# Join of first stage, attention and output projection: conditioning rows, casts and multiplications moved between engines in a two-layer hybrid backbone

## The chip, the core and the metric

The kernel runs on one core of one Trainium2 chip. The core has five engines, each with its own instruction stream: TensorE (PE) multiplies matrices and loads their stationary operands (PEld), VectorE (DVE) does element-wise work and reductions, ScalarE (ACT) does copies, casts and activation functions, GpSimd (POOL) does element-wise work too, and SyncE (SP) mostly starts transfers (DMA). The engines wait for each other through semaphores. The metric is the device time of one execution in microseconds (us), as the median over runs.

## The reference

The function is a two-layer backbone over 2048 latent tokens (a grid of 32 x 64) and 256 context tokens, 1024 channels wide. Cut to what matters here, one layer is:

```python
shift, scale, gate = jnp.split(silu(c) @ w_ada[l] + b_ada[l], 3, axis=-1)   # conditioning, latent and context
hx = rmsnorm(x, norm_w[l]) * (1.0 + scale) + shift
(fx, fgx, nq, nk, nv, ng, gq, gk, gv, gg, zf, zb) = jnp.split(hx @ w_in[l], IN_SPLITS, axis=-1)
four_x = fourier_mix(fx, w_four[l])                       # 4 groups, real part of a 2-D DFT, a linear map
na_x = neighbourhood_attention(nq, nk, nv, nkc, nvc, rpb) # 6 heads, window 8 x 16, and all context keys
gla_x = ...                                               # 4 heads of gated linear attention, both directions
mix_x = concatenate([four_x * silu(fgx), na_x * silu(ng), gla_x * silu(gg)])
x = x + gate * (mix_x @ w_out[l])
```

Context tokens go through the same weights with their own conditioning in the first layer. A last RMSNorm follows the second layer. All inputs are float32. The kernel works in pairs of float16 numbers instead: a value is split into its rounded half (high) and the rest (low), and a product is the sum of the multiplications of the halves.

## The kernel before, in words

**Stages.** A layer has a Fourier stage, an attention stage (`na`), a stage of gated linear attention and an output projection. Weights and conditioning of later stages are prepared in small steps in between. In the first layer a start-up comes ahead of them (from L1660 on): it computes the conditioning, normalises the tokens, two tiles of 128 tokens (a *pair*) at a time, and multiplies each pair by the first two groups of the input weights, `fx` (values of the Fourier group) and `fg` (their gate).

**Order.** Nearly all instructions are issued through `Pin` (L64), which keeps an engine's instructions in the order in which the program issues them; L72 is its line, so nearly every row of a profile bears L72, and instructions are told apart by the names of their tiles. The order of the code is thus the order on each engine, and an engine waits at the instruction whose operand is late, with all later ones behind it.

**Banks.** PE writes into banks of 128 x 512 numbers, of four kinds with two buffers each, named `b_a`, `b_b`, `b_c` and `b_pj`.

**Conditioning (`ada`, L131).** The product `silu(c) @ w_ada` is done in chunks of 256 columns, each with its own weight block of 1 MB. For a chunk PE does eight multiplications, one for each 128 input channels, with a stationary operand of two columns (latent and context), `sil`. They lie in four groups of rows of one bank, 0, 32, 64 and 96, two rows each, so the result is the sum over four groups of rows. In the start-up `mm_r` does the multiplications and `fin_r` the rest: ACT copies the first two rows to `ada_row`, DVE adds the other three groups, PE transposes the row into columns by two small multiplications with `ident`, and DVE adds the bias columns `bc`. In the first layer's attention stage the same is done for the second layer by `chunk`: there the steps are `s0` (loads of weights and of the bias row), `s1` (multiplications), `s1b` (four DVE additions) and `s2` (transposes and a copy). Chunks 0 to 7 give shift and scale; chunks 8 to 11 give the gate and are stored as rows.

**Weights (`w_steps`, L468).** A group of input weights is prepared in steps: a load, four reductions to the largest magnitude (`red`), a multiplication by `dg` that spreads this maximum over all rows (`mm`, `top_b`), its reciprocal (`inv`), and then four slices each of the high and the low halves (`hi` on ACT, `lo` on DVE). `sc` says whether the factors that depend on the conditioning are computed at the end as well.

**A pair in the start-up.** `norm_a` squares and sums on ACT, `norm_b` scales the tokens, `put_t` turns them with 16 small multiplications by `ident` into the banks b and c, and `put_e` evacuates these with the conditioning into `hu`, on ACT and at two of eight places on DVE, then splits `hu` into the high (DVE) and low (POOL or DVE) halves of `hx`. `four_x` and `four_g` multiply `hx` by a group of weights, 48 multiplications a pair of the first size.

**Attention.** A *unit* is a pair of heads and a block of 512 latent queries (or the 256 context queries): three head pairs, with five blocks in the first layer and four in the second, 27 units in all. A unit is a list of steps that `fill` (L889) puts in order: each step gets a due time between 0 and 1 and the list is sorted by it. In a unit stand, among others:

- the scores of each piece, `score`: multiplications `b_a<-q,k` and `b_a<-Q,K`, a DVE step that adds the position bias (`pt`), and behind it, as `flush` in the list, the exponential on ACT (`pt<-pt,psh`), its cast to the high half `ph` on ACT and the low half `pl` on POOL; then `value`, the multiplications `b_c<-ph,vt` and `b_c<-pl,vt`;
- for the next unit the projection of the queries and `st_q`, whose `cast` makes the high halves on DVE and the low halves `q` on POOL;
- for the next unit the row maxima `st_m`: multiplications `k,q` in the banks a and b, a DVE maximum `MX` each, then the maxima's halves `mh`, and in `fin` (L729) 16 small multiplications with `mh` into a bank b, which are cast into two query operands `Q`, 64 x 512 each: the first (h = 0) on ACT, the second (h = 1) on DVE;
- for the unit before its `tail` (L757): the reciprocals of the row sums with three transfers (`rc<-rs`, `rrd<-rc`, `rs<-rrd`), and as its last step two POOL multiplications, `gt<-gt,rs` and `ob<-ob,gt`, and a store;
- side jobs (`side`): weights of later groups, the second layer's conditioning in the first layer, and `wo_scale`, the maximum of the output weights.

## Time and profile before

| what | value |
|---|---|
| median of 3 runs | 2481.02 us (2479.67 to 2491.21) |
| the profiled execution's own time | 2481.09 us |
| its span in the trace | 2479.3 us |
| mean granted clock of PE | 0.979 of full speed |
| instructions of PE, DVE, ACT, POOL | 16878, 3625, 2049, 1285 |

The durations in the rows further down come from one profiled execution, whose time lies 0.07 us from the median. Busy time is the time in which an engine works on an instruction; PE's loads of stationary operands run beside its multiplications and are counted apart. A multiplication's end is modelled, so rows of PE can overlap by fractions of a microsecond. The granted clock says at which share of full speed PE ran in a stretch: 1.0 is 2.4 GHz, 0.5 is 1.2 GHz.

### The profile page before, as it was taken

To read this page: it belongs to the slowest core of one execution; us is meant where nothing else is said; L and a number is where in the kernel's file an instruction comes from. 1 tells how busy PE (TensorE), PEld (TensorE's weight loads), DVE (VectorE), ACT (ScalarE), POOL (GpSimd) and SP (SyncE) were. 2 spreads that over 40 slices of the span, in tenths; PEclk is the share of its full clock that TensorE was granted. 3 is DMA by queue.
4 is the path that set the end of the run, shared out by engine and by line. 5 is a ranking of instruction groups with operands and counts; after the bars stand their busy time and mean duration, and the time that the engine had idled before them with its cause. 6 is when DMAs were issued, how large, how long until landed. Compare 5 with 4: busy or idle time off the path is not lost.

```text
span 2479.3 us, 44404 instructions
## 1 busy us (share of the span) xinstructions
PE 2308.9 (93%) x16878; PEld 1540.2 (62%) x16878; DVE 1623.3 (65%) x3625; ACT 1121.3 (45%) x2049; POOL 1123.5 (45%) x1285
## 2 busy tenths in 40 slices
PE   5999998999978999999999999999999799999998
PEld 3555454454546999895444644555555599989443
DVE  5765766676766666696774627667666666679554
ACT  3623554555555444342332225566666534434222
POOL 1524444455544444454553143655555444445343
PEclk7999999999999999999999999999999999999999
DMA  6304124124221110264443021131320211036442
GB/s 256 119 1 137 64 82 114 62 86 125 75 88 59 44 39 31 99 197 160 145 145 119 19 89 32 46 100 52 83 56 24 73 41 38 31 98 208 147 149 98
DMA packets 128622, 225.05 MB, mean 91 GB/s; under 512 B 18724, under 2 KB 81816, under 8 KB 122776
## 3 DMA queue, kind: packets, MB, share of 16 engines
q1 hardware_dynamic: 123224, 212.58, 25.1%
q0 software_dynamic: 5184, 9.64, 2.6%
q8 instruction: 133, 2.18, 0.4%
q14 instruction: 81, 0.66, 0.1%
HBM read 176.79 MB, written 51.37 MB: 92 GB/s over the span
## 4 chain that ended last, share of the span: by engine, by line
PE 36%; DVE 7%; ACT 3%; issue 2%; POOL 1%; DMA 1%; POOLq 0%; SPq 0%; ACTq 0%; DVEq 0%
PE b_pj L72 18%; PE b_a L72 8%; PE b_c L72 4%; PE b_pj L313 3%; PE b_b L72 2%; DVE ot L72 1%; DVE pt L72 1%; ACT pt L72 1%; DVE SU L72 0%; PE b_a L374 0%; DMA rc<-rs 0%; DVE wo L72 0%; DVE w L72 0%; ACT ph L72 0%; DVE gt L72 0%
## 5 line engine op out<-in xcount | busy, mean ns | idle before, releaser
L72 PE MATMUL b_pj<-hx,w 128*128 128x512 f16 (+1 forms) x3168 | 690.0, 364 | 1.8 <-DVE w L72 0.9
L72 POOL TENSOR_TENSOR pl<-pt,ph 128x512 f16<-128x512 f32 (+6 forms) x300 | 306.6, 1024 | 444.2 <-ACT ph L72 368.7
L72 PEld LDWEIGHTS <-w 128*128 128x128 f16 x3168 | 305.6, 99 | 277.1 <-issue 15.8
L72 PEld LDWEIGHTS <-hx 128*128 128x128 f16 x5088 | 435.6, 99 | 5.5
L72 PE MATMUL b_pj<-w,hx 128*128 128x192 f16 (+2 forms) x4272 | 391.4, 250 | 0.0
L72 PE MATMUL b_pj<-wo,m 128*128 128x512 f16 x816 | 302.7, 380 | 0.0
L72 PE MATMUL b_a<-wo,m 128*128 128x512 f16 x816 | 302.4, 380 | 0.0
L72 PEld LDWEIGHTS <-m 128*128 128x128 f16 x1632 | 160.1, 98 | 184.5 <-issue 1.6
L72 DVE SCALAR_TENSOR_TENSOR pt<-b_a,sc,TS 128x160 f32<-128x160 f32 (+4 forms) x432 | 153.0, 400 | 136.9 <-PE b_a L72 99.9
L72 ACT ACTIVATE pt<-pt,psh 128x480 f32<-128x480 f32 (+1 forms) x192 | 121.6, 633 | 169.1 <-DVE pt L72 156.7
L72 PE MATMUL b_c<-ph,vt 128*128 128x320 f16 (+5 forms) x888 | 179.4, 294 | 3.2 <-ACT ph L72 3.2
L72 PEld LDWEIGHTS <-vt 128*128 128x128 f16 x1332 | 120.7, 100 | 94.6 <-issue 31.7
L72 POOL TENSOR_TENSOR xn<-xn,xt 128x512 f32<-128x512 f32 x66 | 110.3, 1692 | 149.0 <-DVE xn L72 117.6
L72 ACT CAST ph<-pt 128x512 f16<-128x512 f32 (+6 forms) x300 | 166.5, 555 | 9.5
L72 PE MATMUL b_c<-pl,vt 128*128 128x320 f16 (+5 forms) x444 | 126.4, 294 | 9.7 <-POOL pl L72 9.6
L72 PE MATMUL b_a<-Q,K 128*128 128x320 f16 (+5 forms) x444 | 120.7, 294 | 13.1 <-ACT Q L72 13.1
L72 DVE CUSTOM_DVE_ANT_0 b_b<-b_b,tmi 128x512 f32<-128x512 f32 (+3 forms) x144 | 86.4, 600 | 69.5 <-PE b_b L72 68.9
L72 PE MATMUL b_a<-q,k 128*128 128x320 f16 (+5 forms) x444 | 121.2, 295 | 4.7 <-DVE MX L72 2.3
L72 ACT ACTIVATE pt<-b_a,psh,sc 128x512 f32<-128x512 f32 (+1 forms) x108 | 81.1, 750 | 78.7 <-PE b_a L72 67.9
L72 PEld LDWEIGHTS <-q 128*128 128x128 f16 x540 | 51.0, 98 | 81.9 <-issue 21.1
L72 POOL TENSOR_TENSOR ats<-ATm 128x512 f32<-128x512 f32 x34 | 43.3, 1272 | 126.9 <-DVE ATm L72 126.9
L313 PE MATMUL b_pj<-hx,w 128*128 128x512 f16 x432 | 96.8, 379 | 0.0
(272 smaller groups left out, 4212.1 us busy)
## 6 DMA issues: line engine op xcount, KB each, us to landing
mx<-mixd SPq DMA_DIRECT2D x34, 512.0 KB
ws<-in_w_in SPq DMA_DIRECT2D x16, 1024.0 KB
xt<-in_x SPq DMA_DIRECT2D x32, 512.0 KB
ws<-in_w_ada SPq DMA_DIRECT2D x16, 1024.0 KB
ws<-in_w_out SPq DMA_DIRECT2D x16, 1024.0 KB
TS<-in_ts SPq DMA_DIRECT2D x12, 1000.0 KB
xres<-xn SPq DMA_DIRECT2D x18, 512.0 KB
qdt_d<-qkT SPq DMA_DIRECT2D x34, 256.0 KB
```

Source lines behind the costliest of these rows:

```text
L72: return self.tc.keep_in_program_order(f(*args, **kw))
L313: te.matmul(out=pt[:, 0:n], lhsT=w[wi][:, k, c0:c0 + P], rhs=r, start=(k == 0 and z == 0), stop=(k == KB - 1 and z == 2))
```

## The change

The change has six places:

1. *Conditioning of the first layer.* The stationary operand is widened from 2 to 32 columns, 30 of them zero (`silw`). So the multiplications fill all 128 rows of a bank, and one ACT copy of 128 x 256 with two multiplications by a selector `sel` (128 x 2, with ones in the rows of one column) sums the four groups and turns the result. The chunks alternate between banks a and pj.
2. *The weights `fg`.* They are loaded behind the second weight block of the conditioning into a staging tile of their own, `ws2`, and reduced and converted between the chunks; before, that was done between the first pairs. Their conditioning factors follow behind the first pair. The second pair's scaling moves from DVE to ACT, behind the first pair's evacuation, and the first block of multiplications stands ahead of the second pair's turn.
3. *Conditioning of the second layer.* Chunks 0 to 7 get the same form as in 1; their biases come in columns, by one transfer `ada_bc` of 2048 single numbers in place of eight rows.
4. *Casts of the maxima.* In each unit both casts into `Q` are done on ACT, and where an exponential (`flush`) stands directly ahead of them in the list, it is moved behind them.
5. *The tail's last step.* It is put behind the cast of the next query's halves.
6. *`wo_scale`* has three empty steps in place of two ahead of the multiplication that spreads the maximum.

The diff, without the parts that only pass names on:

```diff
+                if c == 0:
+                    lz["silw"] = z = pool.tile([P, 256], F32, tag="row", name="silw1", bufs=1).rearrange("p (k m) -> p k m", k=KB)
+                    v.memset(z, 0.0)
+                    v.tensor_copy(z[:, :, 0:2], sil)
+                    lz["bc"] = bcl = lz["wk"].tile([P, 16], F32, tag="ada_bc", name="ada_bc", bufs=1)
+                    with nc.allow_non_contiguous_dma("bias in columns"):
+                        nc.sync.dma_start(out=bcl, in_=a["b_ada"][l, 0:2048].rearrange("(j p) -> p j", p=P))
+                    lz["sel"] = z = lz["wk"].tile([P, 2], F32, tag="ada_sel", name="sel1", bufs=1)
+                    v.tensor_reduce(out=z, in_=ident.rearrange("p (g c) -> p c g", c=32)[:, 0:2, :], op=ALU.add, axis=AX.X)
+                if c >= 8:
+                    d["row"] = pool.tile([P, 256], F32, tag="row", name="ada_row", bufs=1)[0:2, :]
...
             def s1b():
                 pt = d["pt"]
+                if c < 8:
+                    d["row"] = lz["wk"].tile([P, 256], F32, tag="adar", name="adar", bufs=1)
+                    Pin(tc, S).copy(out=d["row"], in_=pt[:, 0:256])
+                    return
                 for o in range(0, P, 32):
                     v.tensor_tensor(out=d["row"], in0=pt[o:o + 2, 0:256], in1=d["row"], op=ALU.add)
-                if c >= 8:
-                    nc.sync.dma_start(out=gated[l][:, (c - 8) * 256:(c - 7) * 256], in_=d["row"])
+                nc.sync.dma_start(out=gated[l][:, (c - 8) * 256:(c - 7) * 256], in_=d["row"])
 
             def s2():
                 pt = bank("b")
                 for q in range(2):
-                    te.transpose(out=pt[:, 2 * q:2 * q + 2], in_=d["row"][:, q * P:(q + 1) * P], identity=ident[0:2, 0:2])
-                v.tensor_copy(sc[:, :, 2 * c:2 * c + 2], pt[:, 0:4].rearrange("p (q w) -> p w q", w=2))
+                    te.matmul(out=pt[:, 2 * q:2 * q + 2], lhsT=d["row"][:, q * P:(q + 1) * P], rhs=lz["sel"], start=True, stop=True)
+                v.tensor_tensor(out=sc[:, :, 2 * c:2 * c + 2], in0=pt[:, 0:4].rearrange("p (q w) -> p w q", w=2), in1=lz["bc"][:, 2 * c:2 * c + 2].unsqueeze(1).to_broadcast([P, 2, 2]), op=ALU.add)
 
             return [s0, s1, s1b] + ([lambda: None, s2] if c < 8 else [])
...
-        def mm_r(w, te):
-            pt = bank("a")
+        def mm_r(c, w, te, silw):
+            pt = bank(("a", "pj")[c % 2])
             for k in range(KB):
                 o = k % 4 * 32
-                te.matmul(out=pt[o:o + 2, 0:256], lhsT=sil[:, k, :], rhs=w[:, k, :], start=(k < 4), stop=(k >= 4))
+                te.matmul(out=pt[o:o + 32, 0:256], lhsT=silw[:, k, :], rhs=w[:, k, :], start=(k < 4), stop=(k >= 4))
             return pt
 
-        def fin_r(c, pool, pt, bc, te, v, s):
-            row = pool.tile([2, 256], F32, tag="ada_row2", name="ada_row2", bufs=2)
-            s.copy(out=row, in_=pt[0:2, 0:256])
-            for o in range(32, P, 32):
-                v.tensor_tensor(out=row, in0=pt[o:o + 2, 0:256], in1=row, op=ALU.add)
+        def fin_r(c, pool, pt, bc, sel, te, v, s):
+            row = pool.tile([P, 256], F32, tag="ada_row2", name="ada_row2", bufs=2)
+            s.copy(out=row, in_=pt[:, 0:256])
             for q in range(2):
-                te.transpose(out=pt[:, 256 + 2 * q:258 + 2 * q], in_=row[:, q * P:(q + 1) * P], identity=ident[0:2, 0:2])
+                te.matmul(out=pt[:, 256 + 2 * q:258 + 2 * q], lhsT=row[:, q * P:(q + 1) * P], rhs=sel, start=True, stop=True)
             v.tensor_tensor(out=sc[:, :, 2 * c:2 * c + 2], in0=pt[:, 256:260].rearrange("p (q w) -> p w q", w=2), in1=bc[:, 2 * c:2 * c + 2].unsqueeze(1).to_broadcast([P, 2, 2]), op=ALU.add)
...
                     for h in range(2):
                         o = 64 - h * 64
-                        (v.tensor_copy if h else s.copy)(out=Q2s[h, ev][o:o + 64, 0:n], in_=pmt[o:o + 64, 0:n])
+                        s.copy(out=Q2s[h, ev][o:o + 64, 0:n], in_=pmt[o:o + 64, 0:n])
...
+                    late = qcast = y
...
                 if i > 0:
-                    ev += [(min(0.01 + 3.0 * q / T_, 0.09 * q + 0.01), z) for q, z in enumerate(tail(*units[i - 1], ds[i - 1]))]
+                    tl = [(min(0.01 + 3.0 * q / T_, 0.09 * q + 0.01), z) for q, z in enumerate(tail(*units[i - 1], ds[i - 1]))]
+                    qc = [f for f, z in ev if qcast and z is qcast[0]]
+                    ev += tl[:-1] + [(max([tl[-1][0]] + [f + 0.5 / T_ for f in qc]), tl[-1][1])]
                 gaps = [getattr(z, "gap", 0.0) / T_ for z in sd]
                 step = (0.96 - sum(gaps)) / max(1, sum(not z for z in gaps))
                 at = 0.0
                 for z, gp in zip(sd, gaps):
                     ev.append((at, z))
                     at += gp or step
-                return [z for _, z in sorted(ev, key=lambda z: z[0])]
+                ev = [z for _, z in sorted(ev, key=lambda z: z[0])]
+                for z in fs:
+                    k = n = ev.index(z)
+                    while callable(ev[n - 1]) and ev[n - 1] is not flush:
+                        n -= 1
+                    if ev[n - 1] is flush:
+                        ev.insert(k, ev.pop(n - 1))
+                return ev
...
-        return [s0, s1] + ([lambda: None, lambda: None, s1b, s2] if c == 3 else [])
+        return [s0, s1] + ([lambda: None] * 3 + [s1b, s2] if c == 3 else [])
...
+        silw = s0.tile([P, KB, 32], F32, name="silw", bufs=1)
+        V.memset(silw, 0.0)
+        V.tensor_copy(silw[:, :, 0:2], sil)
+        sel = s0.tile([P, 2], F32, name="sel", bufs=1)
+        V.tensor_reduce(out=sel, in_=ident.rearrange("p (g c) -> p c g", c=32)[:, 0:2, :], op=ALU.add, axis=AX.X)
...
-        wg = w_steps(0, "fg", lambda w: W0.__setitem__("g", w), pin=True, tag="pj")
+        wg = w_steps(0, "fg", lambda w: W0.__setitem__("g", w), pin=True, sc=False, tag="pj", lag=2, stage=lambda n: ah.tile([P, n], F32, name="ws2", bufs=1))
...
             def hook(k):
                 if k == 0:
                     norm_b(i + 1)
-                step(wg, 2)
...
         fetch(0)
         step(wx)
-        ws = [load_r(c, ah) for c in range(4)]
+        ws = [load_r(c, ah) for c in range(2)]
+        step(wg)
+        ws += [load_r(c, ah) for c in range(2, 4)]
         norm_a(0)
         norm_b(0)
         put_a(0)
         for c in range(8):
             if c + 4 < 8:
                 ws.append(load_r(c + 4, ah))
-            pts.append(mm_r(ws[c], te))
+            pts.append(mm_r(c, ws[c], te, silw))
             if c:
-                fin_r(c - 1, s0, pts[c - 1], bc, te, v, s)
+                fin_r(c - 1, s0, pts[c - 1], bc, sel, te, v, s)
             step(wx, 2)
+            if c > 1:
+                step(wg, 3)
         fetch(1)
-        step(wg)
         fetch(2)
         step(wx, 99)
-        Wx = W0["x"]
-        fin_r(7, s0, pts[7], bc, te, v, s)
+        step(wg, 99)
+        Wx, Wg = W0["x"], W0["g"]
+        fin_r(7, s0, pts[7], bc, sel, te, v, s)
         ast.close()
         ug[0] = four_pool(fst[0])
         mod(v, s, g, te, "pj")
         Wx["scales"]()
         norm_a(1)
-        norm_b(1)
-        put_e(s0, 0, [pairs[0], pairs[0] + 1], ra[0], V=v, S=s, G=g, hook=lambda k: step(wg, 2))
+
+        def norm_1(k):
+            if k == 3:
+                for q in range(2):
+                    s.activation(out=xs[1][:, q, :], in_=xs[1][:, q, :], func=AF.Copy, scale=rs[1][q])
+
+        put_e(s0, 0, [pairs[0], pairs[0] + 1], ra[0], V=v, S=s, G=g, hook=norm_1)
+        Wg["scales"]()
         fetch(3)
         for n, (f, b) in enumerate(((0, 4), (1, 4), (0, 3), (1, 3), (0, 2), (1, 2), (0, 1), (1, 1), (0, 0)), 1):
-            if n < len(pairs):
-                put_a(n)
-                put_b(n)
+            def put(n=n):
+                if n < len(pairs):
+                    put_a(n)
+                    put_b(n)
+
+            if n > 1:
+                put()
             if f:
                 four_g(ug[0], b, W0["g"], te=te, s=s, v=v)
             else:
                 four_x(ug[0], b, Wx, te=te, s=s)
+            if n == 1:
+                put()
```

The first piece of the order is that of PE in the start-up, from the multiplications of the last conditioning chunk to the first multiplications by `fx` (`b_pj<-hx,w`). Before:

```order
L72 MATMUL b_a<-ada_w,sil 2x256 x8
L72 MATMUL b_a<-ident,ada_row_309 128x2 x2
L72 MATMUL b_a<-ident,ada_row_327 128x2 x2
L72 MATMUL b_pj<-dg,ones 128x128 x2
L72 MATMUL b_b<-ident,xt 128x128 x4
L72 MATMUL b_c<-ident,xt 128x128 x4
L72 MATMUL b_b<-ident,xt 128x128 x4
L72 MATMUL b_c<-ident,xt 128x128 x4
L72 LDWEIGHTS w_241
L72 MATMUL b_pj<-hx,w_241 128x256
```

And in the changed kernel:

```order
L72 MATMUL b_pj<-ada_w,silw 32x256 x8
L72 MATMUL b_a<-sel,ada_row_319 128x2 x2
L72 MATMUL b_pj<-sel,ada_row_332 128x2 x2
L72 MATMUL b_pj<-dg,ones 128x128
L72 LDWEIGHTS w_243
L72 MATMUL b_pj<-hx,w_243 128x256
```

The second `dg` multiplication, that of the `fg` weights, has gone up between the chunks, and the turn of the second pair (`ident,xt`) now stands behind the first block of multiplications.

The second piece is that of ACT in the second layer's first head pair, where the casts into `Q` of a unit stand. Before:

```order
L72 ACTIVATE pt<-pt,psh 128x320
L72 CAST ph<-pt 128x320
L72 ACTIVATE pt<-pt,psh 128x440
L72 CAST ph<-pt 128x440
L72 ACTIVATE w_16675<-ws,wsm 128x512
L72 CAST Q_01_16012<-b_b 64x512
L72 ACTIVATE gt<-b_pj,wsm 128x512
```

And in the changed kernel:

```order
L72 ACTIVATE pt<-pt,psh 128x320
L72 CAST ph<-pt 128x320
L72 ACTIVATE w_16631<-ws,wsm 128x512
L72 CAST Q_01_15968<-b_b 64x512
L72 CAST Q_11_15982<-b_b 64x512
L72 ACTIVATE pt<-pt,psh 128x440
L72 CAST ph<-pt 128x440
L72 ACTIVATE gt<-b_pj,wsm 128x512
```

The exponential of 440 columns and its cast moved behind the casts into `Q`, and the second of these is new on ACT.

The third piece is that of POOL in the second layer where a head pair's first unit follows the last unit of the head pair before; `q` are the low halves of the next unit's queries. Before:

```order
L72 TENSOR_TENSOR pl<-pt,ph 128x480
L72 TENSOR_TENSOR gt<-gt,rs 128x512
L72 TENSOR_TENSOR ob<-ob,gt 128x512
L72 TENSOR_TENSOR q_17397<-qf,q_17397 64x512
L72 TENSOR_TENSOR q_17401<-qf,q_17401 64x512
L72 TENSOR_TENSOR pl<-pt,ph 128x400
L72 TENSOR_TENSOR K_05_16015<-kf,k_17458 64x256
```

And in the changed kernel:

```order
L72 TENSOR_TENSOR pl<-pt,ph 128x480
L72 TENSOR_TENSOR q_17350<-qf,q_17350 64x512
L72 TENSOR_TENSOR q_17354<-qf,q_17354 64x512
L72 TENSOR_TENSOR gt<-gt,rs 128x512
L72 TENSOR_TENSOR ob<-ob,gt 128x512
L72 TENSOR_TENSOR pl<-pt,ph 128x400
L72 TENSOR_TENSOR K_05_15971<-kf,k_17414 64x256
```

The two multiplications of the tail stand behind the two low halves and still ahead of the next `pl` and the key's low half `K`. The order changes in this way at two places of the second layer.

## Rows read from the trace of the kernel before

**Rows 1.** The page's first part: busy time, share of span, instructions.

```profile
PE 2308.9 (93%) x16878; PEld 1540.2 (62%) x16878; DVE 1623.3 (65%) x3625; ACT 1121.3 (45%) x2049; POOL 1123.5 (45%) x1285
```

**Rows 2.** PE's waits: who waits for whom, total us, times, longest us.

```profile
PE b_a L72 <- ACT Q L72: 13.1, 15, 2.1
...
PE b_b L72 <- DVE ada_row L72: 9.4, 7, 2.1
...
PE b_b L72 <- POOL q L72: 9.2, 9, 2.6
```

**Rows 3.** Timeline, start-up: start us, us, engine, instruction, count, idle before and releaser.

```profile
38.98 0.16 DVE L72 TENSOR_TENSOR ada_sc<-b_a,bc 128x4 f32<-128x4 f32 x1 [0.52 <-PE b_a L72]
...
42.80 0.55 ACT L72 ACTIVATE hu<-b_b,modS,modA 128x256 f32<-128x256 f32 x1
...
49.51 0.80 PE L72 MATMUL b_pj<-dg,ones 128*128 128x128 f32 x2 [8.04 <-ACT dg L72]
...
53.51 6.47 PE L72 MATMUL b_pj<-hx,w 128*128 128x256 f16 x48
...
60.86 0.85 ACT L72 ACTIVATE u<-b_pj,wsm 128x256 f32<-128x256 f32 x2
...
63.84 0.55 ACT L72 ACTIVATE hu<-b_b,modS,modA 128x256 f32<-128x256 f32 x1
...
71.79 10.52 PE L72 MATMUL b_pj<-hx,w 128*128 128x512 f16 x48
...
71.84 1.09 ACT L72 ACTIVATE junk<-xt 128x1024 bf16<-128x1024 f32 x1
...
74.11 0.55 ACT L72 ACTIVATE hu<-b_b,modS,modA 128x256 f32<-128x256 f32 x1
...
78.19 0.53 DVE L72 TENSOR_SCALAR hu<-b_b,modA,modS 128x256 f32<-128x256 f32 x1
```

**Rows 4.** Stretches: length, busy us of each engine, PE clock, DMA share, GB/s.

```profile
28.00:32.00 4.00, 3.27 (x32) 1.08 (x35) 3.17 (x8) 0.99 (x2) 0.00 (x0) 0.50 0.96 384
...
52.00:56.00 4.00, 4.00 (x22) 3.28 (x21) 1.37 (x4) 2.49 (x4) 0.90 (x3) 0.54 0.29 80
```

**Rows 5.** Instructions on the tile `ada_row` (ns), and two of PE's rows.

```profile
L72 ACT COPY ada_row<-b_a x8: 345/360/363, 15.5 to 35.8; 2x256 f32<-2x256 f32 x8
...
285.75 0.25 PE L72 MATMUL b_b<-ident,ada_row 2*128 2x2 f32 x2 [2.12 <-DVE ada_row L72]
...
430.91 0.28 PE L72 MATMUL b_b<-ident,ada_row 2*128 2x2 f32 x2 [1.26 <-DVE ada_row L72]
```

**Rows 6.** Timeline, casts into `Q` in the second layer, `pl` in the first.

```profile
1535.71 0.66 ACT L72 ACTIVATE pt<-pt,psh 128x440 f32<-128x440 f32 x1 [3.70 <-DVE pt L72]
...
1537.61 0.58 ACT L72 CAST Q<-b_b 64x512 f16<-64x512 f32 x1
...
1538.24 0.38 PE L72 MATMUL b_a<-Q,K 128*128 128x512 f16 x1 [2.06 <-ACT Q L72]
...
616.74 0.28 PE L72 MATMUL b_c<-pl,vt 128*128 128x280 f16 x1 [0.20 <-POOL pl L72]
```

**Rows 7.** Timeline, the tail's multiplications on POOL, and PE behind them.

```profile
1588.48 1.31 POOL L72 TENSOR_TENSOR gt<-gt,rs 128x512 f32<-128x512 f32 x1
...
1591.22 2.37 POOL L72 TENSOR_TENSOR q<-qf,q 64x512 f16<-64x512 f32 x2
...
1592.42 0.31 PE L72 MATMUL b_b<-k,q 128*128 128x320 f16 x1 [2.61 <-POOL q L72]
...
1593.67 0.94 POOL L72 TENSOR_TENSOR pl<-pt,ph 128x400 f16<-128x400 f32 x1
...
1601.49 0.28 PE L72 MATMUL b_c<-pl,vt 128*128 128x280 f16 x1
```

**Rows 8.** A transfer on the chain that ended last, and SP's issues.

```profile
1579.99 2.22 DMA rc<-rs
...
216.63 10.83 SPq L599 DMA_DIRECT2D k<-k  x6
```

More of the change, by code (lines that the diff above doesn't have):

```diff
@@ L134, in ada @@
         nc.sync.dma_start(out=nw, in_=a["nwcol"][l])
+        lz = {}
         def chunk(c, pool=pool):
@@ L143, in s0 @@
                 nc.sync.dma_start(out=d["w"], in_=a["w_ada"][l, c])
-                d["row"] = pool.tile([P, 256], F32, tag="row", name="ada_row", bufs=1)[0:2, :]
-                nc.sync.dma_start(out=d["row"], in_=a["b_ada"][l:l + 1, c * 256:(c + 1) * 256].to_broadcast([2, 256]))
+                if c == 0:
[9 more added lines that the diff above has]
+                    d["row"] = pool.tile([P, 256], F32, tag="row", name="ada_row", bufs=1)[0:2, :]
+                    nc.sync.dma_start(out=d["row"], in_=a["b_ada"][l:l + 1, c * 256:(c + 1) * 256].to_broadcast([2, 256]))
             def s1():
@@ L150, in s1 @@
                     o = k % 4 * 32
-                    te.matmul(out=pt[o:o + 2, 0:256], lhsT=sil[:, k, :], rhs=d["w"][:, k, :], start=(k < 4), stop=(k >= 4))
+                    if c >= 8:
+                        te.matmul(out=pt[o:o + 2, 0:256], lhsT=sil[:, k, :], rhs=d["w"][:, k, :], start=(k < 4), stop=(k >= 4))
+                    else:
+                        te.matmul(out=pt[o:o + 32, 0:256], lhsT=lz["silw"][:, k, :], rhs=d["w"][:, k, :], start=(k < 4), stop=(k >= 4))
             def s1b():
                 pt = d["pt"]
+                if c < 8:
+                    d["row"] = lz["wk"].tile([P, 256], F32, tag="adar", name="adar", bufs=1)
+                    Pin(tc, S).copy(out=d["row"], in_=pt[:, 0:256])
+                    return
                 for o in range(0, P, 32):
                     v.tensor_tensor(out=d["row"], in0=pt[o:o + 2, 0:256], in1=d["row"], op=ALU.add)
-                if c >= 8:
-                    nc.sync.dma_start(out=gated[l][:, (c - 8) * 256:(c - 7) * 256], in_=d["row"])
+                nc.sync.dma_start(out=gated[l][:, (c - 8) * 256:(c - 7) * 256], in_=d["row"])
             def s2():
@@ L204, in mod @@
             V.tensor_scalar_mul(modS[l], sc[:, :, 0:8], mx[:, 2:3])
-        return chunk, mod, (load_r, mm_r, fin_r)
+        return chunk, mod, (load_r, mm_r, fin_r, lz)
     def rms(pool, xt, junk, S=S, G=G):
@@ L905, in fill @@
                 ms, fs = [], []
-                pre_, scl = [], []
+                pre_, scl, qcast = [], [], []
                 if i + 1 < len(units):
@@ L917, in fill @@
                     push(x)
-                    late = y
+                    late = qcast = y
                     mark["q"] = len(seq) + 2
@@ L937, in fill @@
                 push(st_g(p, b, d))
-                sd = side(p, b, wk)
+                sd = side(p, b, wk, bk)
                 K = len(allp[i])
@@ L1703, in step @@
                     z.pop(0)()
-        chunk0, mod, (load_r, mm_r, fin_r) = ada(0, s0)
+        chunk0, mod, (load_r, mm_r, fin_r, _) = ada(0, s0)
         pairs = list(range(NT - 2, -1, -2))
@@ L1799, in body @@
         if not last:
-            chunk, mod, _ = ada(1, wp)
+            chunk, mod, (_, _, _, lz) = ada(1, wp)
             jobs += [chunk(c) for c in range(8)] + [[lambda: mod(Pin(tc, V), Pin(tc, S), Pin(tc, G), Pin(tc, TE))]]
@@ L1805, in body, with side @@
         pre = {}
-        def side(p, b, wk):
+        def side(p, b, wk, bk):
             n = p + 1
             res = []
+            if not last:
+                lz["wk"] = bk
             if b == 0:
```

## The prediction

> **What bounds the kernel now.** I read the page first: TensorE (PE) is busy 2308.9 us of the span of 2479.3 us [rows 1], and the program around it makes 2481.09 us. The reader is to see that little else can move the time: whatever shortens the run takes away some of the 170 us in which PE stands still, or raises its clock. The list of who waited for whom on PE then says where. Of the waits in the attention stages the three that this change touches are those for the casts of the row maxima (ACT Q), for the conditioning rows of the second layer (DVE ada_row) and for the low halves of the queries (POOL q): 13.1, 9.4 and 9.2 us [rows 2]. Last I read the first 80 us in order of time: PE's first dense block starts at 53.51 us, and from 71.79 us on it runs without a gap [rows 3]. Those 71.79 us are a chain of ACT, DVE and DMA work, so a shorter chain moves all that follows.
>
> **The change part by part.**
>
> *Start-up, conditioning.* Each of eight chunks was reduced by an ACT copy of 2 rows, three DVE additions and two small transposes; now one ACT copy of all 128 rows and two multiplications by a selector do it, and the chunks alternate between two kinds of banks. The last of them ended before at 38.98 + 0.16 = 39.14 us [rows 3]. What bounds it now is the DMA: the engines are full until about 31.6 us (96% of the stretch from 28 to 32) [rows 4], and in that time they bring as much as is needed now before the last chunk: the second weight block has come in, the next latent tiles have moved behind. So the last chunk lands at about 31.6 us, its multiplications take about 1.9 us more, copy, selector and addition about 0.9: 34.4. I add 2 us, since the eight slices of both weight blocks are now converted on ACT and DVE in between (in order, ahead of some of the copies). That gives 36.4, 2.7 us earlier.
>
> *Start-up, fg weights.* Before, their reductions and conversions stood between the token pairs: PE waited 8.04 us for their maximum, to 49.51 us, ahead of its first block [rows 3]. They are now done before the pairs begin. From the end of the conditioning to the first `hu` it takes 42.80 - 39.14 = 3.7 us, so `hu` starts at 40.1, and the first block (48 multiplications, 6.47 us before [rows 3]) about 1.4 us later. It will run slower, partly at the lower clock and partly behind POOL's lows: I take 9.5 us, to 51. Then ACT evacuates it and squares the next pair (from 60.86 to 63.84 before, 3.0 us; I take 3.5), so the next `hu` starts at 54.5. A pair takes ACT 6.5 us without weights in between (squares from 71.84 to 74.11, then `hu` until 78.19 [rows 3]), so the `hu` after it starts at 61. Before, that one started at 63.84. Its last bank comes free 4.1 + 0.5 us later (74.11 to 78.19 plus the instruction, a pair without weights [rows 3]) and PE's turn of the next pair ends 0.7 us after that: the dense run begins at 66.3 instead of 71.79. I take 5.5 us. Bounds: 10 us, if the first block isn't slowed, and nothing, if the clock stays low (first rival).
>
> *Second layer's conditioning.* Eight chunks in the first attention stage: four DVE additions each go, one ACT copy comes. PE waited here six times, first 2.12 us at 285.75 and last 1.26 us at 430.91, together 8.2 us [rows 5] (the rest of the 9.4 us belongs to later chunks, which keep the old form). The copy is no row of this trace; the nearest is the copy of 2 rows, 0.36 us [rows 5], and a cast of 64x512 takes 0.58 us [rows 6]. It can stand behind an exponential and its cast, so from both sides: all 8.2 us go, or eight copies that are each 1.3 us late make it 2.2 us worse. ACT has idle time ahead of most of them (3.70 us in the same place of the second layer [rows 6]), so I take four fifths, 6.6 us.
>
> The eight small loads of biases are replaced by one whose elements are single numbers of 4 bytes, 2048 of them; it stands on SP's queue among the copies `k<-k`. The nearest row is `rc<-rs`, 512 such numbers, 2.22 us [rows 8]: between 2.2 and 8.9 us for it. The first six of these copies take 10.83 us from 216.63 on in any case [rows 8], so I count on most of it being covered: 0 to 3 us, I take nothing. A rule speaks against it: the Trainium skill (DMA: Bandwidth & Descriptors, Rules for kernel authors) says that a non-contiguous last dimension becomes one descriptor per element. By it the higher price holds, and the sum would be up to 3 us longer; no run so far shows this load.
>
> *Cast of the maxima.* In each of 27 units the second cast moves from DVE to ACT, and both now stand ahead of the pending exponential. In the unit at 1538 ACT first waited 3.70 us for DVE, to 1535.71, then did the exponential, its cast and a weight slice, and only at 1537.61 the cast of the maxima, for which PE waited 2.06 us [rows 6]. Now ACT does both casts, 2 x 0.58 us, within those 3.70 us, and the exponential starts on time. So the 13.1 us [rows 2] go but for what comes back elsewhere; I take 85%, 11.1 us. Where DVE has nothing between `mh` and the exponential's input, the exponential comes later; PE already waits 0.20 us for POOL's `pl` at one of these places [rows 6]. I charge 1.5 us for some six such units. Worst: every exponential late by both casts (third rival).
>
> *Multiplications behind the lows.* Twice in the second layer (the unit at 1592 and the same one of the next head pair) POOL did `gt` and `ob` (about 1.3 us each) ahead of the two `q`, and PE waited 2.61 us, to 1592.42 [rows 7]. Exchanged, the first `q` is ready at 1588.48 + 1.2 = 1589.7, and PE comes at 1592.42 - 2.61 = 1589.8. What could be late next is POOL's `pl`, which stands behind all four before and after and so starts near 1593.67 as it did and ends at 1594.6; PE, 2.6 us earlier, asks for it at 1598.9 (1601.49 less 2.6) [rows 7]. It is covered, and 2 x 2.6 us go, at least nothing; I take 4.7.
>
> *Rest.* One more empty step ahead of the output weights' maximum moves one small multiplication of the second layer; no wait stood there. Nothing.
>
> Sum: 5.5 + 6.6 + 11.1 + 4.7 - 1.5 = 26.4 us; 2481.09 - 26.4 = 2454.7. The median of the runs is 2481.02, so no correction: **2455 us**.
>
> **The rivals.**
>
> 1. The start-up gain is eaten by PE's clock. It stands at 0.50 from 28 to 32 us and is 0.54 in the mean of 52 to 56 [rows 4], that is, it comes back to the higher level of the two (1.2 and 2.4 GHz) only at the end of that stretch, after PE worked through from 49.51. In the changed kernel PE starts earlier but with gaps, and stands still again while pair two is normalised. At 2.4 GHz a 512-wide multiplication takes 10.52 / 48 = 0.219 us [rows 3], a 256-wide one half, and at 1.2 GHz 0.219. If the first two blocks run at 1.2 GHz throughout, the first takes 48 x 0.219 = 10.5 us, 1.0 above my 9.5, and the second 48 x 0.11 = 5.3 us longer: 6.3, more than the 5.5 gained. Then 2461. The Trainium skill (TensorE: Matmul & The Clock Gate, What's actually happening) has the throttled state as the default that activity releases; this trace agrees.
> 2. The waits move instead of vanishing. PE also waits for MX, mh and pl, which come from the same engines; if half of 6.6 + 11.1 + 4.7 comes back there, 11.2 us are left of it: 2481.1 - 5.5 - 11.2 + 1.5 = 2466. Against it: in the unit at 1538 no other engine is late then.
> 3. ACT becomes the bound of the attention units, and the run is slower. Both casts, 2 x 0.58 = 1.16 us, stand ahead of an exponential in 27 units. If every exponential comes that much later and PE waits for each, 27 x 1.16 = 31.3 us are added, and the copies of the second layer's conditioning stand behind late casts as well (2.2 us worse). The 13.1 us for Q still go, and start-up and lows still give 5.5 + 4.7 = 10.2: 31.3 + 2.2 - 13.1 - 10.2 = 10.2 us slower, 2491. It decides from (13.1 + 10.2 - 2.2) / 27 = 0.78 us of delay a unit. For it speaks the 0.20 us at 616.74, against it the 3.70 us in which ACT stands still [rows 6].
> 4. The change doesn't do what it says: the named wait for Q is put down to the last releaser, and the casts stay behind something else. Then 11.1 is missing: 2466.
>
> **How the numbers follow.** Chances: forecast 0.62, rivals 0.14, 0.12, 0.05 and 0.05, and 0.02 for the load of biases at 2458. The forecast's own span is 2444 to 2464. All gains at their bounds (10 + 8.2 + 13.1 + 5.2 = 36.5), with 2 us of higher clock, make 2442; up to 2471 the range takes in rivals 1, 2 and 4 with 5 us above them. About 0.5% (12.4 us) can be told from no change: faster means under 2468.6. The forecast, 0.12 of rival 1, 0.07 of 2, 0.02 of 4 and the load make 0.85; slower 0.03 of rival 3; 0.12 between.
>
> **What would show it.** Right: PE's waits for ACT Q and for `adar` under 4 us together; the unit at 1538 without a wait before `Q,K`; POOL q near 4 us; the run of 512-wide multiplications from about 66 us. Wrong: a first block that is dense no earlier than 70 us, waits for `pl` or `ph` that grow by more than 5 us, or PE's busy time growing by as much as its idle time falls, at a lower clock.

## The result and the profile after

The changed kernel takes 2447.01 us (median of 4 runs, 2445.64 to 2454.44) against 2485.01 us for the kernel before on the same chip (4 runs; 2485.27 over 18 runs in a later set). The ratio is 0.9847, 95% interval 0.9815 to 0.9879: 30 to 46 us faster. Forecast were 2455 us and 26.4 us. The profiled execution's span fell from 2479.3 to 2443.5 us, by 35.8.

The first part of the page after, and the line on packets of the page before and of the page after:

```profile
PE 2307.1 (94%) x16910; PEld 1546.7 (63%) x16910; DVE 1582.4 (65%) x3546; ACT 1136.1 (46%) x2086; POOL 1121.4 (46%) x1285
```
```profile
DMA packets 128622, 225.05 MB, mean 91 GB/s; under 512 B 18724, under 2 KB 81816, under 8 KB 122776
```
```profile
DMA packets 130653, 225.04 MB, mean 92 GB/s; under 512 B 20772, under 2 KB 83848, under 8 KB 124808
```

PE's busy time is the same within 2 us [rows 1], but only as a sum. Up to the 512-wide run [rows 3] it grew by 6.7 us (from 40.5 to 47.2). From there on it fell by 8.5 and the idle time by 26.6, as the whole of the rest shows before and after (length, busy us of PE, PEld, DVE, ACT and POOL, PE clock, DMA share, GB/s):

```profile
71.79:2479.30 2407.51, 2268.43 (x16570) 1513.62 (x16567) 1578.96 (x3522) 1091.24 (x1987) 1105.25 (x1257) 0.99 0.27 86
```
```profile
71.13:2443.50 2372.37, 2259.93 (x16586) 1513.48 (x16583) 1547.63 (x3464) 1103.02 (x2021) 1103.43 (x1257) 0.99 0.28 87
```

The packets under 512 bytes grew by 2048: the load of 2048 single numbers is one packet each.

PE's waits after (releaser, total us, times, longest):

```profile
PE b_b L72 <- DVE xt L72: 14.7, 4, 9.3
...
PE b_c L72 <- POOL pl L72: 11.8, 20, 2.6
...
PE b_b L72 <- POOL q L72: 4.2, 7, 1.1
...
PE b_a L72 <- ACT Q L72: 1.6, 3, 1.0
...
PE b_b L72 <- DVE ada_row L72: 1.2, 1, 1.2
...
PE b_b L72 <- ACT adar L72: 0.3, 1, 0.3
```

The three waits of [rows 2] fell by 11.5, 8.2 and 5.0 us (what is left for `ada_row`, 1.2, is a later chunk in the old form; the new copy `adar` brings 0.3). The one for `pl` grew by 2.2 (9.6 before), and the one for `xt`, which belongs to the start-up, by 4.2 (10.5 before).

The unit that stood at 1538 [rows 6], now at 1518 (first ACT, then PE):

```profile
1516.44 1.18 ACT L72 CAST Q<-b_b 64x512 f16<-64x512 f32 x2 [1.44 <-PE b_b L72]
1518.08 0.66 ACT L72 ACTIVATE pt<-pt,psh 128x440 f32<-128x440 f32 x1 [0.45 <-DVE pt L72]
```
```profile
1518.17 0.38 PE L72 MATMUL b_a<-q,k 128*128 128x512 f16 x1
1518.39 0.38 PE L72 MATMUL b_a<-Q,K 128*128 128x512 f16 x1
```

Here ACT does both casts in time in which it waited for DVE's `pt` before, and still waits 0.45 us for it; PE has no wait ahead of `Q,K`. And the place of [rows 7] (POOL, then PE):

```profile
1568.84 2.38 POOL L72 TENSOR_TENSOR q<-qf,q 64x512 f16<-64x512 f32 x2
1571.30 1.27 POOL L72 TENSOR_TENSOR gt<-gt,rs 128x512 f32<-128x512 f32 x1
```
```profile
1570.05 0.31 PE L72 MATMUL b_b<-k,q 128*128 128x320 f16 x1
```

The wait of 2.61 us is gone. The start-up is the surprise; PE's rows of it, and DVE's last addition of the conditioning:

```profile
20.14 1.93 PE L72 MATMUL b_a<-ada_w,silw 128*32 128x256 f32 x16 [2.35 <-DMA ada_w<-in_w_ada]
...
35.24 1.01 PE L72 MATMUL b_pj<-sel,ada_row 128*128 128x2 f32 x4
36.19 1.93 PE L72 MATMUL b_pj<-ada_w,silw 128*32 128x256 f32 x16
38.05 1.01 PE L72 MATMUL b_a<-sel,ada_row 128*128 128x2 f32 x4
...
46.02 0.40 PE L72 MATMUL b_pj<-hx,w 128*128 128x256 f16 x1 [2.97 <-DVE hx L72]
...
59.31 0.30 PE L72 MATMUL b_b<-ident,xt 128*128 128x128 f32 x1 [3.28 <-DVE xt L72]
60.78 0.79 PE L72 MATMUL b_b<-ident,xt 128*128 128x128 f32 x3 [1.17 <-DVE xt L72]
...
71.13 9.23 PE L72 MATMUL b_pj<-hx,w 128*128 128x512 f16 x42
```
```profile
40.58 0.15 DVE L72 TENSOR_TENSOR ada_sc<-b_pj,bc 128x4 f32<-128x4 f32 x1
```

The 512-wide run starts at 71.13 instead of 71.79 [rows 3]: 0.7 us, not 5.5. The conditioning ends at 40.7 us, later than before (39.1). PE stood still for 2.35 us ahead of the third weight block, and its granted clock, 1.00 from 16 to 20 us, is 0.50 from 20 us until 50.7.

**A part that no wait shows.** Three stretches of 4 us in the first layer's attention, before and after at the same places of the program (columns as in [rows 4]):

```profile
412.00:416.00 4.00, 3.06 (x14) 1.47 (x14) 2.59 (x9) 1.69 (x3) 3.06 (x4) 0.76 0.36 81
430.00:434.00 4.00, 3.09 (x14) 1.93 (x15) 2.77 (x8) 2.27 (x5) 0.71 (x1) 0.64 0.48 140
472.00:476.00 4.00, 2.73 (x9) 1.59 (x10) 2.15 (x9) 2.18 (x6) 1.15 (x1) 0.51 0.78 262
```
```profile
404.00:408.00 4.00, 3.37 (x23) 1.86 (x22) 2.72 (x9) 2.72 (x6) 3.77 (x6) 1.00 0.52 212
420.00:424.00 4.00, 3.24 (x36) 2.25 (x37) 1.58 (x6) 3.06 (x6) 0.73 (x2) 1.00 0.92 334
460.00:464.00 4.00, 3.04 (x20) 1.86 (x21) 2.76 (x8) 3.30 (x7) 1.27 (x2) 1.00 0.57 231
```

The third number from the end is the granted clock. Before, PE fell to 1.2 GHz behind waits for `ada_row` (412, 431) and behind a wait of 0.77 us for `Q` and one of 2.79 us for `dg` (472). After, it stays at 2.4 GHz, though a wait of 2.46 us for `dg` at 461 and two for `mh` at 419 and 420 are still there. I added up, over stretches of 1 us from 75 us on, PE's busy time multiplied by what the clock lacked to 1.0: 30.1 us are lost so in the profile before, 23.1 after. The three places make 1.7 + 1.7 + 2.8 = 6.2 of the 7.0 us. Both sums come from one execution each; what other executions show follows behind the experiments.

That makes the account: PE's waits from 81 us on fell by 26.4 us, the start-up gave 0.7, the clock 7.0, together 34.1 of 35.8. The 8.5 us by which PE's busy time fell are the clock's 7.0 and 1.5 more, which lie in the 1.7 that are left.

### The profile page after: what moved, and what is told of

The parts are those of the page before. It is cut to its first block, busy times and chain, and to the rows that moved or that the text cites. A ratio compares the mean times of both kernels' runs of the same rounds, so it can differ in the third digit from the quotient of the medians.

```text
span 2443.5 us, 44388 instructions
## 1 busy us (share of the span) xinstructions
PE 2307.1 (94%) x16910; PEld 1546.7 (63%) x16910; DVE 1582.4 (65%) x3546; ACT 1136.1 (46%) x2086; POOL 1121.4 (46%) x1285
## 5 line engine op out<-in xcount | busy, mean ns | idle before, releaser
L72 ACT ACTIVATE pt<-b_a,psh,sc 128x512 f32<-128x512 f32 (+1 forms) x108 | 80.9, 749 | 62.5 <-PE b_a L72 52.0
```

The costliest lines, as they stand in the source:

```text
L72: return self.tc.keep_in_program_order(f(*args, **kw))
```

## The experiments

Each kernel was timed beside the kernel before on its chip; a difference in us is the ratio applied to that kernel's median. "Clock-free" is the span less the time lost at 1.2 GHz counted as above (before 2479.3 - 30.1 = 2449.2; after 2443.5 - 23.1 = 2420.4): it takes out that one execution has more such stretches than another. It rests on one profiled execution of each kernel.

**One part at a time.** First the rows alone (shortened):

```diff
+    Pin(tc, S).copy(out=d["row"], in_=pt[:, 0:256])      # chunks 0 to 7, then two multiplications by sel
-    for o in range(0, P, 32): v.tensor_tensor(out=d["row"], ...)
...
```

> The kernel before with the new form of the second layer's conditioning alone (one ACT copy and selector multiplications for chunks 0 to 7, biases in columns). Theory A (a removed wait also takes away a stretch at 1.2 GHz behind it): PE's waits for the rows fall by 8.2 us, the stretches from 410 to 420 and from 430 to 440 us, which stood at a granted clock of 0.83, go back to 1.00 and give 1.7 us each: 11.6 us faster, all of it between 240 and 440 us; the stretch at 470 stays below 1.0. Theory B (a wait is worth what its row says): 8.2 us faster, PE busy time unchanged. Theory C (the new copies on ACT or the load of 2048 single numbers give the gain back): under 4 us.

Measured: ratio 0.9945 (0.9928 to 0.9962), 9 to 18 us; clock-free 7.5. The waits for rows fell by 8.2 us. Matched instruction by instruction with the kernel before, this one is 10.2 us ahead at 440 us and level with it up to 240: more than the waits alone (theory B, 8.2), less than theory A's 11.6. The stretches at 1.2 GHz behind them are gone, the one behind `Q` and `dg` has stayed, as theory A has it:

```profile
404.00:408.00 4.00, 3.37 (x27) 2.21 (x26) 2.62 (x9) 3.49 (x7) 3.69 (x5) 1.00 0.61 246
...
422.00:426.00 4.00, 4.00 (x35) 2.52 (x27) 2.02 (x5) 3.66 (x7) 1.40 (x2) 1.00 0.93 337
461.00:465.00 4.00, 1.92 (x7) 1.23 (x8) 2.12 (x13) 2.00 (x5) 0.52 (x1) 0.58 0.63 215
```

But the profiled execution, the slowest of the four, lost 36.7 us at 1.2 GHz in all, more than before: at other places such stretches came that no edit explains, and at its end it is only 0.9 us ahead. The mean granted clock of the other three executions was 0.980 or 0.981, that of this one 0.975.

The casts alone (shortened):

```diff
-    (v.tensor_copy if h else s.copy)(out=Q2s[h, ev]..., in_=pmt...)
+    s.copy(out=Q2s[h, ev]..., in_=pmt...)
+    # in fill: a flush directly ahead of fin moves behind it
```

> The kernel before with the casts of the maxima alone: both on ACT, and ahead of the exponential that stood directly before them. Theory A: PE's waits for Q fall by 11.5 us, waits for pl grow by 2, and the stretch at 470 to 480 us, which had a wait of 0.77 us for Q and 2.79 us for dg close together and then ran at 1.2 GHz, stays at 1.00 and gives 2.7 us more: 12 us faster, 4 of it in the first layer, 8 in the second. Theory B (waits alone): 9.3 us, 470 to 480 still below 1.0. Rival 3 of the prediction (ACT late): under 4 us.

Measured: 0.9923 (0.9907 to 0.9939), 15 to 23 us; clock-free 17.5. Waits for `Q` fell from 13.1 to 1.6 us, `pl` grew by 1.9. Not foreseen: the waits for the old rows fell by 5.4 us too, since DVE, which adds those rows, has 27 casts less. Of these 1.4 came back: ahead of the transposes of one row (427.57 us) PE waits 1.36 us still, only put down to ACT's cast `Q` now, where it was 1.26 us for the row before (430.91, [rows 5]). So 4.0 us are gone. All of PE's waits from 81 us on fell by 16.2 us, so the gain lies above both theories (12 and 9.3) by waits. Theory A's own sign didn't come: the clock still falls at all three places, at the last one by less (1.7 us lost, 2.8 before):

```profile
410.00:414.00 4.00, 4.00 (x16) 1.89 (x17) 1.23 (x5) 1.39 (x2) 2.23 (x3) 0.61 0.66 205
427.00:431.00 4.00, 3.43 (x15) 2.00 (x16) 1.79 (x6) 2.80 (x5) 0.73 (x2) 0.61 0.46 131
468.00:472.00 4.00, 3.34 (x14) 1.99 (x15) 2.70 (x7) 2.61 (x5) 1.15 (x1) 0.61 0.54 229
```

The tail alone (its last step behind the cast of the next query):

> The kernel before with the tail's last step behind the next query's lows alone. Theories A and B: PE's waits for POOL q fall from 9.2 to about 4 us, in the second layer's attention alone: 5 us faster, nothing elsewhere. Rival (pl becomes late in its place): under 2 us, with pl's waits 3 us higher.

Measured: 0.9971 (0.9961 to 0.9981), 5 to 10 us; clock-free 6.5. Waits for `q` fell from 9.2 to 4.0 us, those for `pl` grew by 1.3: the term is right in size.

The start-up alone:

> The kernel before with the start-up's changes alone (selector form of the first layer's conditioning, fg weights early, second pair's scaling on ACT, first block ahead of its turn). Theory A (the start-up gains nearly nothing by itself: PE at 1.2 GHz takes 2.9 us a chunk): the run of 512-wide multiplications starts 0.7 us earlier than 71.79 us, and the run is 0.7 us faster. The prediction's theory (5.5 us, hidden in the whole change by something else): 66 us and 5.5 us faster.

Measured: 0.9987 (0.9977 to 0.9997), 1 to 6 us; the 512-wide run starts at 70.92 us, 0.9 earlier; clock-free 3.0. The interval of the time would just admit 5.5 us, the start of the run doesn't: they aren't hidden elsewhere, they never came.

Clock-free the four parts give 7.5 + 17.5 + 6.5 + 3.0 = 34.5 us, the whole change 28.8. Of the difference, 5.7, 4.0 us are waits for rows that both the first and the second take away; the rest is not explained, and each figure rests on one execution.

**Place or engine.** The casts' two halves, `s.copy` for both without the move, and the move with the second cast left on DVE:

> The kernel before with the second cast of the maxima on ACT, but both casts left behind the exponential. If the place ahead of the exponential is what counts, PE's waits for Q stay above 10 us of 13.1, and what is left is relief of DVE (27 casts less), which takes some of the waits for the conditioning rows: 3 to 5 us faster. If the engine is what counts (DVE's cast was late), the waits for Q fall under 4 us and the run is 12 us faster or more.

> The kernel before with the exponential moved behind the casts of the maxima, the second cast left on DVE. If the place counts: waits for Q fall from 13.1 to under 4 us, the waits for the conditioning rows stay near 9.4, and the run is 10 us faster. If the engine counts: waits for Q stay above 9 us, under 4 us faster.

Measured: 0.997 (0.9958 to 0.9983), 4 to 10 us, and 0.9941 (0.992 to 0.9961), 10 to 20 us. PE's waits, first with the engine changed, then with the place:

```profile
PE b_a L72 <- ACT Q L72: 13.2, 15, 2.1
...
PE b_b L72 <- DVE ada_row L72: 4.1, 4, 1.4
```
```profile
PE b_c L72 <- POOL pl L72: 12.9, 18, 2.5
...
PE b_b L72 <- DVE ada_row L72: 6.2, 6, 1.4
...
PE b_a L72 <- ACT Q L72: 1.8, 3, 1.0
```

The place takes the wait for `Q` (13.1 to 1.8 us). The engine takes nothing of it (13.2): its gain is DVE's relief, 5.3 us of the waits for rows, less the 1.4 that come back as above. But the place alone, with the second cast still on DVE, took 3.2 us of the waits for rows as well (9.4 to 6.2), where none was expected; why is not shown.

**The start-up's halves.** The selector form alone, and the whole of place 2 of the change (early fg weights, second pair's scaling on ACT, first block ahead of the second pair's turn) with the old form. Each was run once, for its profile:

> The kernel before with the selector form of the first layer's conditioning alone, the fg weights left between the pairs. Theory: in the changed kernel a chunk costs PE 2.9 us at 1.2 GHz (16 rows of multiplications 1.93, selector 1.01, instead of 0.34 for the transposes), and the fg block ahead of the third chunk delays it by 2.4 us. Without the fg block the conditioning then ends at 37 us (39.9 in the changed kernel, 39.1 before), and the 512-wide run starts at about 70 us, since PE still waits for the fg weights' maximum. If transfers alone set it, the third weight block comes at 17.7 us and the conditioning ends by 35 us.

> The kernel before with the fg weights early and the first block ahead of the second pair's turn, the old form of the conditioning kept (copy of two rows, three additions, transposes). Theory: the fg block ahead of the third chunk delays it by 2.4 us, and DVE has additions and conversions to do in order: the conditioning ends at 41.5 us, and the 512-wide run starts at 72.5 us, later than before (71.79). If the selector form is what holds the changed kernel back, the conditioning ends before 39 us and the run starts before 70 us.

Measured: the form alone ends the conditioning at 36.3 us and starts the 512-wide run at 68.93; place 2 alone ends it at 45.7 and starts the run at 77.18. PE's row of the first and a row of DVE of the second:

```profile
68.93 10.52 PE L72 MATMUL b_pj<-hx,w 128*128 128x512 f16 x48
```
```profile
45.50 0.16 DVE L72 TENSOR_TENSOR ada_sc<-b_a,bc 128x4 f32<-128x4 f32 x1 [0.53 <-PE b_a L72]
```

So the form gives 2.9 us and place 2 takes back 2.2. With the old form it costs 5.4, more than I expected: DVE's three additions a chunk stand in order among the conversions, and PE waits for them six times behind 25 us, 0.9 to 3.0 us each.

**Better start-ups.** Three variants of the changed kernel: without place 2; with the third pair scaled in the hole behind the first pair; and with the weights reduced in that hole, spread behind the first block.

```diff
# second variant (shortened)
         put_e(s0, 0, [pairs[0], pairs[0] + 1], ra[0], V=v, S=s, G=g, hook=norm_1)
         Wg["scales"]()
+        norm_a(2)
+        norm_b(2)
...
# third variant (shortened), besides: the load of fg behind fetch(1), and
+        step(wg, 4)          # reductions, ahead of norm_a(2)
+            if n == 1:
+                step(wg, 3)  # behind the first block; conversions in put_b's hook
```

> The changed kernel with the early fg weights undone (loaded, reduced and converted between the pairs as before, second pair's turn ahead of the first block); the selector form and all the rest kept. The early fg weights cost more than they give: the 512-wide run starts at 69 us instead of 71.1, 2 us faster than the changed kernel, about 2445 us. If they pay in the presence of the rest: 1 us slower or more than the changed kernel.

> The changed kernel with the third pair's squares (ACT) and scaling (DVE) put right behind the first pair's evacuation, into the hole in which both engines wait for the first block. If the first block's place is what the third pair's scaling makes dear (PE waited 3.28 and 1.17 us for xt behind it): the waits for xt go, the second pair's evacuation starts at 55 instead of 56.9 us, and the 512-wide run starts at 67 instead of 71.1 us: 4 us faster than the changed kernel. If PE waits for the second pair's halves anyway: 1 us.

> The changed kernel with the fg weights loaded where they were before (behind the conditioning's blocks), reduced on DVE while PE is at the first block, spread behind that block and converted beside the second pair; with the third pair's scaling early as well. The conditioning then ends at 36.3 us (39.9 in the changed kernel), and the 512-wide run starts at 66 us: 5 us faster than the changed kernel, 2442 us. If ACT, which has four slices of weights and two pairs to do by then, holds it: 69 us, 2 us faster.

Measured: 2449.53, 2446.81 and 2449.35 us, ratios 0.985, 0.9844 and 0.985, each within 0.0025, the changed kernel's 0.9847. The 512-wide run starts earlier in all three, PE's rows in that order:

```profile
68.18 10.52 PE L72 MATMUL b_pj<-hx,w 128*128 128x512 f16 x48
```
```profile
68.38 10.52 PE L72 MATMUL b_pj<-hx,w 128*128 128x512 f16 x48
```
```profile
67.32 10.52 PE L72 MATMUL b_pj<-hx,w 128*128 128x512 f16 x48
```

The first variant shows what holds the conditioning of the changed kernel. A stretch of the changed kernel and the same of the variant, and the variant's last chunk:

```profile
20.00:24.00 4.00, 3.86 (x26) 2.15 (x30) 0.87 (x3) 0.48 (x2) 0.00 (x0) 0.50 1.02 424
```
```profile
20.00:24.00 4.00, 3.40 (x42) 2.10 (x42) 0.84 (x5) 0.80 (x3) 0.00 (x0) 1.00 1.01 424
```
```profile
31.53 1.94 PE L72 MATMUL b_pj<-ada_w,silw 128*32 128x256 f32 x16 [0.69 <-DMA ada_w<-in_w_ada]
```

Its PE waits 0.37 us for the third weight block, not 2.35, and its clock stays at 2.4 GHz until 30.2 us, where a chunk costs PE 1.07 + 0.61 = 1.7 us. From the third chunk on it waits five times for weight blocks, 3.7 us in all, and the conditioning ends at 35.5 us. With the form alone the clock fell at 23.4 us, and the end was 36.3: the clock is part of what place 2 costs, but not tied to it alone.

Matched instruction by instruction, the first and the third are still 3.0 and 3.3 us ahead of the changed kernel's profile at 560 to 640 us and even with it at 740; the second, 2.7 ahead at 180, had lost its lead by 480, 1.7 us of it at 1.2 GHz from 459 us on. Between 640 and 740 (the changed kernel, the third variant, and the kernel of the next experiment, whose first layer is the changed kernel's own) the clock was lower in all profiles of this set than in the changed kernel's:

```profile
640.00:740.00 100.00, 85.34 (x559) 48.58 (x557) 64.44 (x176) 59.76 (x103) 49.29 (x48) 0.97 0.26 87
```
```profile
640.00:740.00 100.00, 86.44 (x541) 48.42 (x540) 63.42 (x173) 57.38 (x99) 47.01 (x47) 0.91 0.24 78
```
```profile
640.00:740.00 100.00, 86.92 (x542) 48.92 (x541) 62.02 (x166) 57.95 (x98) 47.07 (x46) 0.90 0.27 86
```

The last of them, with the changed kernel's own first layer, lost as much, so the variants didn't cause it. Whether 3 to 4 us are left in the time stays open: the intervals are 6 us wide either way, and none of the three is shown to beat the changed kernel.

**What a wait costs.** The changed kernel with each cast into `Q` of the second layer done three times:

```diff
+    for _ in range(3 if last else 1):
         s.copy(out=Q2s[h, ev][o:o + 64, 0:n], in_=pmt[o:o + 64, 0:n])
```

> The changed kernel with each cast of the maxima done three times in the second layer, so that ACT is about 1.8 us later in its 12 units; the value cast is the same. It measures what a wait of PE costs. Theory A (a wait can take the clock down for a stretch behind it): the span grows by the added waits and by 1.7 us, or a multiple, at each place where the granted clock falls; with 1 us of wait a unit, 12 us of waits and 5 to 10 us more. Theory B: it grows by the added waits alone, and the time lost at 1.2 GHz between 1480 and 1890 us stays at nothing.

Measured: 2481.36 us, ratio 0.9977 (0.9964 to 0.999): nearly the whole gain is gone. The second layer's attention in the changed kernel and here, and PE's waits here in all:

```profile
1474.00:1889.00 415.00, 404.87 (x2598) 225.32 (x2596) 281.02 (x798) 263.74 (x432) 226.93 (x235) 1.00 0.21 59
```
```profile
1478.00:1924.00 446.00, 416.72 (x2620) 228.88 (x2618) 282.67 (x799) 289.12 (x477) 227.42 (x235) 0.98 0.21 55
```
```profile
PE b_c L72 <- POOL pl L72: 16.0, 26, 2.2
PE b_c L72 <- ACT ph L72: 14.9, 14, 1.7
```

It grew by 31.0 us: waits by 19.5 (9.5 to 29.0), and PE's busy time by 11.9 for the same work. Of that, 8.3 us lie in five stretches at 1.2 GHz (from 1488, 1529, 1570, 1730 and 1890 us, about 1.7 each); the changed kernel had none there up to 1889. The rest, 3.6, isn't explained. Theory A holds: here 1 us of wait cost 1.6. The waits are for the exponential (`ph`, `pl`), not for `Q`: that is the mechanism of rival 3, at a delay that the change itself doesn't make.

**The clock in other executions.** Are the 7.0 us only the difference of two single executions? The three places of the first layer say no. In the eight profiles of kernels whose second layer's rows have the old form, PE waits for 1.36 us at the place of 412 us and for 1.26 to 1.36 at that of 431, and the clock falls behind the second wait in all and behind the first in seven; in the six with the new form both waits are gone and it falls at neither. At the third place (472) it falls in all eight of the first, and in two of the six. The mean granted clock of every execution says the same: the span times what it lacks to 1.0 is 58.0 us on average over 18 executions of the kernel before, 48.9 over four of the changed kernel; in the set of the three variants it is 62.5 (15 executions of the kernel before) against 51.8, 48.0 and 46.0 (five each). These counts hold the start-up and PE's idle time too.

## Why the prediction was right, and where not

- *Cast of the maxima*: 11.1 forecast, 11.5 measured. The reason given (the cast stood behind the exponential) is shown by moving the place alone. That the cast came to ACT has another effect, not forecast: DVE's relief alone takes 4.0 us of the waits for rows.
- *Second layer's conditioning*: 6.6 forecast, 8.2 measured in waits, though 4.0 of it the casts alone would have taken; the load of 2048 numbers cost nothing that a wait shows, though it was one packet per number. The row taken as the nearest to it, `rc<-rs`, moves its 512 numbers in rows of eight, so the bounds of 2.2 and 8.9 us had no like row behind them.
- *Lows*: 4.7 forecast, 5.0 measured. *Adverse*: 1.5 forecast, 2.2 measured, for `pl` as named.
- *Start-up*: 5.5 forecast, 0.7 measured. Two steps failed.
  The first is the bound of the conditioning. I let the transfers start the last chunk at 31.6 us and charged nothing for the fg block ahead of the third weight block. PE waits 2.35 us for that block, to 20.14, and works at 1.2 GHz from there on, where a chunk takes it 2.9 us (1.93 for the multiplications, 1.01 for the two multiplications by the selector, which are four rows of the trace, where two transposes took 0.34). From 28.84 on it works without a gap worth naming, and the last chunk starts at 36.19 us. What comes behind was right: 4.5 us to the end at 40.7 against 1.9 + 0.9 + 2. Without place 2 the forecast's bound holds: the last chunk starts at 31.53 us and waits for its block. Of the 4.3 us by which the conditioning is late, 2.4 are left at the second pair's `hu` (56.92 us, forecast 54.5).
  The second is the third pair. I let its scaling go free, and I let ACT alone set the way from its `hu` to the 512-wide run, 5.3 us. PE waits 3.28 + 1.17 us for the scaling, its clock falls again in this standstill (0.62 from 60 to 64 us), and it is in the second block until 69.5 us: from `hu` at 63.35 to the run it takes 7.8 us. That is the other 2.5 us; with this scaling early (second of the better start-ups) the run starts 2.75 us earlier.
- *Clock*: the missing term, 7.0 us. I had the clock as a danger of the start-up alone (rival 1). That a wait of about 1 us can cost 1.7 us more behind it stood in the trace, in the lower clock at 412, 431 and 472 us.

That the whole came out near the forecast is partly luck: a term 4.8 us too large and a missing one of 7.0 stand against each other. Of the four signs of being right, three came (1.9 us for ACT `Q` and `adar` together, no wait ahead of `Q,K`, 4.2 us for POOL `q`); the fourth, the run from about 66 us, didn't.

Rival 1's loss came (no start-up gain), and the clock has a share in it, but not where rival 1 put it: the first two blocks took PE 7.3 and 5.6 us, not 10.5 each; the clock cost time in the conditioning and in the third pair's turn. Rivals 2 and 4 are refuted by the waits, which came back only with 2.2 us; rival 3 by PE's waits for `pl` and `ph`, 14.8 us after and 12.8 before. The span fell by 9.4 us more than forecast: 4.8 less at the start-up, 1.6 more in the terms above, 7.0 by the clock, 2.7 by waits for `dg` and `MX` in the first layer that fell besides; of the other 2.9, 1.2 are small waits and 1.7 stay unexplained.

## What to carry to other kernels

Where a short cast stands in order behind a long operation that has to wait for another engine, move it into that wait; here the place took 11.3 of 13.1 us of waits, the engine none. Before counting a wait at its own length, look at the granted clock behind it. Before calling a stage bound by its transfers, add up what each piece costs the engine at the clock that it has there.

## What was not expected of the hardware

PE's clock falls in each profile at 9 to 17 places between 75 us and the last microseconds, for 23 to 38 us in all, and most places cost 1.4 to 1.7 us, the others 1.9 to 5.7. Several places come in every kernel (at 1002 to 1026 us and 2163 to 2204 us), others in some executions only, so that single profiles differ by several microseconds with no edit behind it. A stationary operand of 32 columns instead of 2 costs PE almost nothing: 1.93 us for the 16 rows of a chunk at 1.2 GHz, 1.89 before; its loads took 0.16 to 0.17 us each instead of 0.08, beside the multiplications. Of the 1.01 us for the selector at 28.84 us, PE's loads of the stationary operand (128 columns) take up 0.93.
